# Three sets of norm scales loaded at the start into one 48-row tile and turned by one transpose

## The chip, the cores and the metric

The kernel runs on one core of one Trainium2 chip. The metric is the device time of one execution in microseconds (us); for the kernel before it is the median of three runs. Beside them stands one more execution that the hardware profiler recorded, and every duration, wait and queue below is from that one.

The core has five engines that run their own instruction streams and wait for each other by semaphores: PE (TensorE, matrix products and transposes; its weight loads are shown apart as PEld), DVE (VectorE), ACT (ScalarE), POOL (GpSimd) and SP (SyncE, which here issues nearly all loads). A transfer is issued by an instruction on SP or ACT and then carried by the core's 16 DMA engines.

## The reference

The kernel computes two layers of a decoder trunk for one sequence of 256 tokens, width 1024, in float32. Each layer is

```
h = x + 1/2 * SwiGLU_1(RMSNorm(x) * g1)
h = h + mixer(RMSNorm(h) * g2)      # three attention groups, one combined projection
y = h + 1/2 * SwiGLU_2(RMSNorm(h) * g3)
```

`RMSNorm(x) * g` is `x * rsqrt(mean(x*x) + 1e-6) * g`, with a scale vector `g` of 1024 numbers. There are three such vectors for each layer, named `ffn1_norm`, `mix_norm` and `ffn2_norm`, each an array of 2 x 1024 for the two layers. The hidden width of each SwiGLU is 2816. The mixer takes the normalised rows through a projection, attends in 4 + 4 + 8 heads of width 64, and projects back.

## The kernel before, in words

**Layout.** The trunk `h` stays in SBUF as `trunk`, with tokens on the 128 partitions, in two halves of 128 tokens. For a product the activations must lie with the 1024 columns on the partitions. `Norm` does that: for each block of 128 columns PE transposes the two token halves into a PSUM bank (`turn`, L338; in the first layer's opening a `turn` of its own, L495), ACT writes the rounded high part to `xhl` while it multiplies by the norm scale (`Norm.high`, L327), and DVE writes the remainder of it (`Norm.low`, L330). The row factor `rsqrt(...)` is applied later, behind the product.

**The scales.** After the transpose a scale belongs to a partition, so ACT and DVE take it as one number per partition from `gT`, a tile of 128 partitions and 48 columns: column `16 * which + 8 * layer + block`. To get there, `load_gains` (L175) loads one of the three arrays as 16 rows of 128 numbers (two layers by eight blocks) into a temporary tile, and `turn_gains` (L179, L180) transposes these rows on PE into a PSUM bank and copies 16 columns into `gT` on DVE.

**Weights.** Weights are loaded in 1 MB pieces into `raw` (L92, five buffers), split by ACT into a high part `wh` (L118) and by DVE into a low part `wl` (L122), both of type float32r. Every product then is three matmuls: high by high, high by low, low by high (L303). The issue of a load waits on SP until its `raw` buffer is free.

**A feed-forward block** (`ffn`) runs over 22 tiles of 128 hidden columns. Each tile f has a gate and an up product, held by a `Pair` in two PSUM banks of the tag `gu`. There are four banks of that tag, given out in turn. ACT and DVE drain them (L441, L442), and DVE and ACT compute the gated value (L446, L448, L465, L466, L453, L456, L459). The down product of tile f - 4 runs between the products of tile f. Odd and even tiles take their wide (high) and narrow (low) matmuls in opposite order, so that the narrow matmuls of one even tile and of the next odd tile stand beside each other on PE.

**Order.** The program is scheduled by hand: each engine executes its instructions in the order in which the Python code emits them. Semaphores are inserted by the framework from the tiles that instructions read and write.

**The start.** On PE the order is: six warm-up products on a tile of ones (`warm_up(WARM)`, 12 matmuls in the trace), the first transpose of scales (`turn_gains(0)`), the four transposes of the first 256 columns of x (`turn(0)`), three more warm-up products (`warm_up(BRIDGE)`), and then the first products of `opening`, which take the weights in quarter and half pieces as they arrive. On SP the loads are issued in the order x columns 0 to 255, the first quarter of the gate weights, the first of the up weights, x columns 256 to 511, and so on. ACT issues one load, `ffn1_norm`, and then loads its table and runs an `Exp` on a tile of ones (L195), so that the table is there when it is needed.

**The other two sets.** `load_small` is called at tile f = 4 of the first feed-forward block and puts four loads on SP: the constants, `mix_norm`, `ffn2_norm` and the forget bias. `before_mixer`, called at f = 8 behind the products of that tile, turns the two sets by two transposes, each with its own `gu` bank, ahead of the narrow matmuls of f = 9, and puts two copies into `gT` on DVE, ahead of a few more small preparations for the mixer.

The tiles `rows` come from the pool `tmp`, nine buffers that the feed-forward blocks use for their intermediate values; a buffer is given out again when its last use is past.

Of the kernel before, what the change touches and what calls it, by code (L numbers as in the profile page):

```python
# [18 lines left out]
P = 128  # L19
# [123 lines left out]
def kernel(ctx: ExitStack, tc: tile.TileContext, x, ffn1_norm, ffn1_w_gate, ffn1_w_up, ffn1_w_down,  # L143
                      mix_norm, w_in, forget_bias, a_q_norm, a_k_norm, b_q_norm, b_k_norm, c_q_norm, c_k_norm,
                      w_out, ffn2_norm, ffn2_w_gate, ffn2_w_up, ffn2_w_down, const, out):
    nc = tc.nc
# [12 lines left out]
    V, A, G, T = nc.vector, nc.scalar, nc.gpsimd, nc.tensor  # L159

    def bank(tag):
        return psum.tile([P, 512], F32, name="ps_" + tag, tag=tag)

    def tmp(n):
        return tp.tile([P, 512], F32, name="tmp", tag="tmp")[:, :n]
# [2 lines left out]
    trunk = xp.tile([P, 2, D], F32, name="trunk")  # L168
    cst = cp.tile([P, 512], F32, name="cst")
    ident = cp.tile([P, P], F32, name="ident")  # L170
    rows = [tmp(P)[:16] for _ in range(3)]
    gT = cp.tile([P, 48], F32, name="gT")

    def load_gains(i, g, eng):
        eng.dma_start(rows[i], g.rearrange("l (k p) -> (l k) p", p=P))  # L175

    def turn_gains(i):
        ps = bank("gu")
        T.transpose(ps[:, :16], rows[i], ident[:16, :16])  # L179
        V.tensor_copy(gT[:, 16 * i:16 * i + 16], ps[:, :16])  # L180

    ones = cp.tile([P, P], F32, name="ones")
    G.memset(ones, 1.0)  # L183
# [5 lines left out]
    def load_x(mp):  # L189
        cols = slice(256 * mp, 256 * mp + 256)  # L190
        nc.sync.dma_start(trunk[:, :, cols], x[0].rearrange("(t p) d -> p t d", p=P)[:, :, cols])

    load_x(0)
    load_gains(0, ffn1_norm, nc.scalar)
    A.activation(tmp(P), ones, AF.Exp)  # L195

    def head_gains(l):
# [81 lines left out]

    def load_small():  # L280
        nc.sync.dma_start(cst, const)
        load_gains(1, mix_norm, nc.sync)
        load_gains(2, ffn2_norm, nc.sync)
        nc.sync.dma_start(fb, bass.AP(tensor=forget_bias.tensor, offset=forget_bias.offset,
                                      ap=[[0, P], [8, DEPTH], [1, 8]]))

# [94 lines left out]
    def ffn(norm, nxt, aside=None, first=False):  # L381
# [189 lines left out]
        for f in range(1, NF):  # L571
# [32 lines left out]
            if f == 4 and first:  # L604
                load_small()
# [37 lines left out]
    def mixer_tables(l):  # L643
        gb = head_gains(l)
        for i in range(4):
            g = gb[:, i]
            if i % 2 == 0:
                G.tensor_tensor(gq, g, eighth, op=ALU.mult)
                g = gq
            gs = g[:, None, :].to_broadcast([P, 2, HD])  # L650
            G.tensor_tensor(tab[:, i, 0], cs[:, :, 0:64], gs, op=ALU.mult)
            G.tensor_tensor(tab[:, i, 1, :, 0:32], cs[:, :, 64:96], gs[:, :, 32:64], op=ALU.mult)
            G.tensor_tensor(tab[:, i, 1, :, 32:64], cs[:, :, 96:128], gs[:, :, 0:32], op=ALU.mult)
        G.tensor_tensor(gc, gb[:, 4], gb[:, 5], op=ALU.mult)
        G.tensor_tensor(gc, gc, eighth, op=ALU.mult)
# [528 lines left out]

    def before_mixer(l):
        if l == 0:
            turn_gains(1)
            turn_gains(2)
            V.tensor_copy(identr, ident)
            V.memset(causal[:, P:2 * P], 0.0)  # L1190
            for t in range(2):
                V.tensor_scalar(causal[:, 2 * t * P:(2 * t + 1) * P], future, NEG, None, op0=ALU.mult)
        mixer_tables(l)
# [6 lines left out]

    warm_up(WARM, True)
    norm = Norm(0, 0)
    turn_gains(0)
    for l in range(DEPTH):
        norm = ffn(norm, lambda: Norm(1, l), lambda: before_mixer(l), l == 0)
        norm = mixer(l, norm, lambda: Norm(2, l))
        norm = ffn(norm, (lambda: Norm(0, l + 1)) if l + 1 < DEPTH else None)
# [35 lines left out]
```

## Time and profile before

| | |
|---|---|
| median of three runs | 1037.53 us (1037.35 to 1038.41) |
| the profiled execution, own time | 1037.25 us |
| its span, first to last instruction | 1035.5 us |
| PE busy | 1031.3 us, 5641 matmuls |
| DVE busy | 808.0 us |
| ACT busy | 592.1 us |
| POOL busy | 147.3 us |
| moved by DMA | 181.61 MB, mean 175 GB/s |

The profiled execution's own time is 1.75 us longer than its span, which covers what lies ahead of the first and behind the last instruction. In the timeline a row gives start, length, engine, line, operation, the tile written and the tiles read, and in brackets how long the engine had been idle and what ended that. An engine name with a q at its end (SPq, ACTq) is the instruction that issues a transfer, not the transfer. PEld rows are weight loads, which run ahead of the matmul they belong to. Matmuls are pipelined: the start of the next one, not the end of the last, tells the pace.

### The profile page before, as it was taken

What the parts mean: (1) busy time and instruction counts of PE and PEld (TensorE: products, weight loads), DVE (VectorE), ACT (ScalarE), POOL (GpSimd) and SP (SyncE); (2) the same over time, 40 slices, a digit from 0 to 9 for tenths busy, and PEclk for the clock granted to TensorE, in tenths of its full rate; (3) what the DMA queues carried; (4) which work ended last, traced back from release to release, by engine and by line L of the source; (5) the groups of instructions that cost most, each with busy time, mean ns of one, the idle gap of its engine ahead of it and who ended that gap; (6) DMA issues with size and microseconds to landing.
All of it is one profiled execution on the core that took longest, in us unless ns stands there. A gap on an engine that the chain in (4) does not pass through costs nothing.

```text
span 1035.5 us, 15082 instructions
## 1 busy us (share of the span) xinstructions
PE 1031.3 (100%) x5641; PEld 898.4 (87%) x5641; DVE 808.0 (78%) x1537; ACT 592.1 (57%) x1045; POOL 147.3 (14%) x177
## 2 busy tenths in 40 slices
PE   9999999999999999999999999999999999999998
PEld 8888888898888888888888888888988988888887
DVE  6977778789876877777788777787898768777776
ACT  6655556666854655555465555557676646555552
POOL 2003000167800000000000110002766000000000
PEclk9999999999999999999999999999999999999999
DMA  9664656554431364645645564664455224564631
GB/s 324 224 240 162 208 188 198 182 191 170 158 127 42 123 230 150 230 168 203 198 163 193 182 224 146 241 186 172 164 195 170 83 69 160 180 204 162 236 130 41
DMA packets 130808, 181.61 MB, mean 175 GB/s; under 512 B 7040, under 2 KB 104624, under 8 KB 130736
## 3 DMA queue, kind: packets, MB, share of 16 engines
q1 hardware_dynamic: 130704, 180.66, 51.3%
q8 instruction: 44, 0.72, 0.3%
q14 instruction: 28, 0.23, 0.1%
q10 hardware_dynamic: 32, 0.01, 0.0%
HBM read 179.60 MB, written 1.05 MB: 174 GB/s over the span
## 4 chain that ended last, share of the span: by engine, by line
PE 100%; DVE 0%; POOL 0%; issue 0%; POOLq 0%
PE ps_gu L303 66%; PE ps_acc L303 30%; PE ps_acc L338 1%; PE ps_gu L1037 1%; PE ps_gu L1140 1%; PE ps_acc L738 0%; PE ps_acc L1037 0%; PE ps_gu L1070 0%; PE ps_acc L495 0%; PE ps_acc L364 0%; PE ps_acc L1070 0%; PE ps_gu L179 0%; DVE trunk L377 0%; POOL ones L183 0%; POOL minus_half L185 0%
## 5 line engine op out<-in xcount | busy, mean ns | idle before, releaser
L122 DVE TENSOR_TENSOR wl<-raw,wh 128x1024 fp32r<-128x1024 f32 (+2 forms) x342 | 417.0, 1225 | 24.7 <-ACT wh L118 24.7
L118 ACT CAST wh<-raw 128x1024 fp32r<-128x1024 f32 (+2 forms) x341 | 343.1, 1036 | 5.4 <-PE ps_gu L303 4.8
L303 PE MATMUL ps_gu<-xhl,wh 128*128 128x512 f32 x1408 | 330.2, 390 | 0.0
L303 PEld LDWEIGHTS ps_gu<-xhl,wh 128*128 128x128 f32 x1408 | 262.7, 188 | 53.8 <-ACT wh L118 0.3
L303 PEld LDWEIGHTS ps_gu<-xhl,wl 128*128 128x128 f32 x1408 | 176.0, 191 | 4.3 <-issue 0.2
L303 PE MATMUL ps_gu<-xhl,wl 128*128 128x256 f32 x1408 | 179.2, 283 | 0.1
L303 PE MATMUL ps_gu<-wh,xhl 128*128 128x512 f32 (+2 forms) x512 | 157.2, 377 | 0.0
L442 DVE TENSOR_TENSOR tmp<-ps_gu,tmp 128x256 f32<-128x256 f32 x176 | 73.0, 423 | 107.8 <-ACT tmp L441 107.5
L303 PE MATMUL ps_acc<-wh,hh 128*128 128x512 f32 (+1 forms) x352 | 137.2, 390 | 0.0
L303 PE MATMUL ps_acc<-wl,hh 128*128 128x512 f32 (+1 forms) x352 | 137.0, 389 | 0.0
L303 PE MATMUL ps_acc<-wh,hl 128*128 128x512 f32 (+1 forms) x352 | 136.5, 388 | 0.0
L441 ACT COPY tmp<-ps_gu 128x256 f32<-128x256 f32 x176 | 63.5, 371 | 93.5 <-PE ps_gu L303 93.2
L303 PEld LDWEIGHTS ps_gu<-wh,xhl 128*128 128x128 f32 x512 | 94.8, 188 | 14.6
L456 ACT CAST hh<-tmp 128x256 fp32r<-128x256 f32 x80 | 32.6, 407 | 119.7 <-DVE tmp L453 119.7
L303 PE MATMUL ps_gu<-wl,xhl 128*128 128x512 f32 (+2 forms) x256 | 95.7, 374 | 0.0
L448 ACT ACTIVATE tmp<-tmp 128x256 f32<-128x256 f32 x88 | 36.9, 419 | 82.3 <-DVE tmp L446 81.9
L314 POOL TENSOR_TENSOR y_n<-msq,minus_half 128x2 f32<-128x2 f32 x6 | 6.8, 1141 | 530.9 <-DVE msq L313 530.9
L303 PEld LDWEIGHTS ps_acc<-wh,hl 128*128 128x128 f32 x352 | 66.1, 188 | 13.9
L303 PEld LDWEIGHTS ps_acc<-wh,hh 128*128 128x128 f32 x352 | 66.2, 188 | 12.6
L303 PEld LDWEIGHTS ps_acc<-wl,hh 128*128 128x128 f32 x352 | 66.2, 188 | 12.2
L303 PEld LDWEIGHTS ps_gu<-wl,xhl 128*128 128x128 f32 x256 | 48.2, 188 | 6.7
L327 ACT ACTIVATE xhl<-ps_acc,gT 128x256 fp32r<-128x256 f32 x48 | 19.1, 474 | 38.7 <-PE ps_acc L338 35.6
(221 smaller groups left out, 1000.4 us busy)
## 6 DMA issues: line engine op xcount, KB each, us to landing
raw<-in_ffn_w_down_dram SPq DMA_DIRECT2D x44, 1024.0 KB, 4.9
raw<-in_ffn_w_gate_dram SPq DMA_DIRECT2D x42, 1024.0 KB, 6.6
raw<-in_ffn_w_up_dram SPq DMA_DIRECT2D x42, 1024.0 KB, 7.3
raw<-in_w_in_dram SPq DMA_DIRECT2D x24, 1024.0 KB, 4.9
raw<-in_w_out_dram SPq DMA_DIRECT2D x8, 1024.0 KB, 4.9
raw<-in_w_in_dram SPq DMA_DIRECT2D x4, 768.0 KB, 4.9
raw<-in_w_in_dram SPq DMA_DIRECT2D x4, 656.0 KB, 3.9
raw<-in_ffn_w_gate_dram SPq DMA_DIRECT2D x3, 512.0 KB, 7.0
```

Of the source, the lines that this page charges most:

```text
L118: self.nc.scalar.copy(hv, src)
L122: (engine or self.nc.vector).tensor_tensor(lv, self.srcs[self.n_low], hv.bitcast(F32), op=ALU.subtract)
L303: T.matmul(o, l, r, start=start, stop=stop, skip_group_check=True)
L314: G.tensor_tensor(y, dst, minus_half[:, :n], op=ALU.pow)
L327: A.activation(self.h[:, m], src, AF.Copy, scale=gT[:, self.col + m:self.col + m + 1])
L338: T.transpose(ps[:, i, t * P:(t + 1) * P], trunk[:, t, (2 * mp + i) * P:(2 * mp + i + 1) * P], ident)
L441: A.copy(o, ps[:, 1])
L442: V.tensor_tensor(o, ps[:, 0], o, op=ALU.add)
L448: A.activation(th, t_, AF.Tanh, scale=0.5)
L456: (V.tensor_copy if late else A.copy)(hh, t_)
L1037: T.transpose(b[:, j * P:(j + 1) * P], pj[i][:, j * P:(j + 1) * P], ident)
L1140: T.transpose(b[:66, i * S + t * P:i * S + (t + 1) * P], src[t][:, 2 * hp_ + i, :], ident)
```

## The change

The three temporary tiles of 16 rows become one of 48 rows. All three loads are issued by ACT at the start, one behind the other, ahead of the table load. One transpose of 48 rows and one copy of 48 columns take the place of three of each, at the place of the first. The two loads in `load_small` and the two turns in `before_mixer` go away.

```diff
-    rows = [tmp(P)[:16] for _ in range(3)]
+    rows = tmp(P)[:48]
     gT = cp.tile([P, 48], F32, name="gT")

     def load_gains(i, g, eng):
-        eng.dma_start(rows[i], g.rearrange("l (k p) -> (l k) p", p=P))
-
-    def turn_gains(i):
+        eng.dma_start(rows[16 * i:16 * i + 16], g.rearrange("l (k p) -> (l k) p", p=P))
+
+    def turn_gains():
         ps = bank("gu")
-        T.transpose(ps[:, :16], rows[i], ident[:16, :16])
-        V.tensor_copy(gT[:, 16 * i:16 * i + 16], ps[:, :16])
+        T.transpose(ps[:, :48], rows, ident[:48, :48])
+        V.tensor_copy(gT, ps[:, :48])
...
     load_x(0)
-    load_gains(0, ffn1_norm, nc.scalar)
+    for i, g in enumerate((ffn1_norm, mix_norm, ffn2_norm)):
+        load_gains(i, g, nc.scalar)
     A.activation(tmp(P), ones, AF.Exp)
...
     def load_small():
         nc.sync.dma_start(cst, const)
-        load_gains(1, mix_norm, nc.sync)
-        load_gains(2, ffn2_norm, nc.sync)
...
         if l == 0:
-            turn_gains(1)
-            turn_gains(2)
             V.tensor_copy(identr, ident)
...
-    turn_gains(0)
+    turn_gains()
```

## The prediction

> **What bounds the kernel now.** I read the profile's page first: the engines' busy times and the chain that ended last.
>
> ```profile
> span 1035.5 us, 15082 instructions
> ...
> PE 1031.3 (100%) x5641; PEld 898.4 (87%) x5641; DVE 808.0 (78%) x1537; ACT 592.1 (57%) x1045; POOL 147.3 (14%) x177
> ...
> PE 100%; DVE 0%; POOL 0%; issue 0%; POOLq 0%
> ```
>
> PE is busy in 1031.3 of 1035.5 us and the chain is PE from end to end. So a wait anywhere else costs nothing by itself; what counts is how late PE starts, how long it stands, and how many instructions it has. The change touches PE at two places only, and the first one is the start. The timeline of the first microseconds:
>
> ```profile
> 0.78 0.46 ACTq L175 DMA_DIRECT2D tmp<-in_ffn_norm_dram  x1
> ...
> 0.79 0.43 SPq L191 DMA_DIRECT2D trunk<-in_x_dram  x1
> ...
> 1.04 2.93 PE L303 MATMUL ps_gu<-ones 128*128 128x128 f32 x12 [1.04 <-POOL minus_half L185]
> ...
> 1.27 1.28 ACT L195 ACT_TABLE_LOAD   x1 [1.27 <-PEq L1231]
> 1.27 0.46 SPq L92 DMA_DIRECT2D raw<-in_ffn_w_gate_dram  x1
> ...
> 1.78 0.46 SPq L92 DMA_DIRECT2D raw<-in_ffn_w_up_dram  x1
> ...
> 2.56 0.31 ACT L195 ACTIVATE tmp<-ones 128x128 f32<-128x128 f32 x1
> ...
> 3.90 0.18 PEld L179 LDWEIGHTS ps_gu<-ident,tmp 16*128 16x128 f32 x1 [0.22 <-issue]
> ...
> 4.11 0.71 PEld L495 LDWEIGHTS ps_acc<-ident,trunk 128*128 128x128 f32 x4
> ...
> 4.22 0.17 DVE L180 COPY gT<-ps_gu 128x16 f32<-128x16 f32 x1 [4.22 <-PE ps_gu L179]
> 4.60 0.61 POOL L478 CAST wh<-raw 128x512 fp32r<-128x512 f32 x1 [2.88 <-DMA raw<-in_ffn_w_gate_dram]
> ...
> 4.84 0.90 ACT L327 ACTIVATE xhl<-ps_acc,gT 128x256 fp32r<-128x256 f32 x2 [1.97 <-PE ps_acc L495]
> ...
> 5.35 0.91 DVE L330 SCALAR_TENSOR_TENSOR xhl<-ps_acc,gT,xhl 128x256 fp32r<-128x256 f32 x2 [0.95 <-ACT xhl L327]
> ...
> 5.95 0.76 PEld L303 LDWEIGHTS ps_gu<-xhl,wh 128*128 128x128 f32 x4
> ```
>
> Read it from PE. The warm-up products (1.04) are there to fill the time until data arrive. The weight load of the scale transpose follows at 3.90, that of the x transposes at 4.11. ACT takes the first x block at 4.84, when its transposes are through, DVE adds the low part at 5.35, and the first product starts at 5.95. Each of these steps stands behind the transpose of the scales in PE's queue, so what holds that transpose holds everything. When did its data come? The views of the loads, of the transpose's own line, and of the tile `trunk` (whose last line gives the time from issue to landing of its four loads) say:
>
> ```profile
> tmp<-in_ffn_norm_dram ACTq DMA_DIRECT2D x1, 8.0 KB, 2.5
> tmp<-in_mix_norm_dram SPq DMA_DIRECT2D x1, 8.0 KB, 6.5
> tmp<-in_ffn_norm_dram SPq DMA_DIRECT2D x1, 8.0 KB, 6.2
> ```
>
> ```profile
> L179 PEldq EVENT_SEMAPHORE  x3: 51/51/51, 3.4 to 69.6; - x3
> ```
>
> ```profile
> DMA to landing us min/median/max: 3.0/5.3/5.7
> ```
>
> The scales issued at 0.78 landed 2.5 us later, at 3.28; PE's semaphore wait for them ended from 3.40 to 3.45, 0.17 us behind the landing. The first x block, with the shortest of the four landings, 3.0, came at 0.79 + 3.0 = 3.79. Both were there when the warm-up was done. The scale load is covered by the warm-up and by x, with 3.90 - 3.45 = 0.45 us to spare.
>
> The second place is the pair of turns at tile f = 8. The chain of waits in order of time, around the opening and around that place (start, length, what):
>
> ```profile
> 4.18 1.04 PE ps_acc L495 x4
> ...
> 7.66 0.44 PE ps_acc L495 x4
> ...
> 53.45 3.83 PE ps_gu L303 x32
> ...
> 70.01 1.91 PE ps_gu L303 x16
> 71.92 0.22 PE ps_gu L179 x2
> 72.14 2.11 PE ps_gu L303 x16
> ```
>
> The row of 53.45 is the narrow matmuls of tiles f = 6 and 7, 32 of them in 3.83 us. At f = 8 and 9 the same 32 stand in two rows with the two scale transposes between: 70.01 to 74.25 is 4.24 us. The two turns cost 0.41 us of PE there: 0.22 for themselves, and 0.20 by which the 16 matmuls behind them take 2.11 instead of 1.91.
>
> **The change part by part.**
>
> *Three loads at the start.* SP issues its loads 0.48 to 0.51 apart (0.79, 1.27, 1.78). ACT at the same pace would issue its three at 0.78, 1.28 and 1.79, and the one transpose now waits for the third. For its time to land the nearest row is the 2.5 us of the same size on the same queue at the same stage. The far end is the 6.5 us of the same size on SP's queue, behind a megabyte of weights. Between them lies the first quarter of the gate weights, 32 times the bytes: issued at 1.27, used by POOL at 4.60, at most 3.3. I take 2.6, near the row that is nearest, a little more because the DMA engines are busier than when the first load went out. The third set lands at 1.79 + 2.6 = 4.39, PE can go at 4.39 + 0.17 = 4.56, and that is 0.66 later than 3.90. The spare 0.45 is already used in this. With 2.5 it would be 0.56, with 3.3 it would be 1.36.
>
> *What is queued behind that wait.* On PE the four x transposes and all the products: they shift by the 0.66, since x (3.79) is there by then and is no longer what is late. On DVE the copy into `gT` and the low parts, on ACT the high parts; these follow PE. The weight splits on POOL and ACT hang on DMA instead and keep their times.
>
> *ACT's own queue.* Two more issues push the table load and the Exp by 1.79 - 0.78 = 1.01 us: the table load from 1.27 to 2.28, the Exp's end from 2.87 to 3.88. ACT's next instruction comes at 4.84 (then 5.5) after 1.97 us of idling. Cost nothing; if the cover were gone it would be up to 1.01.
>
> *One transpose of 48 rows.* Its matmul has 48 columns instead of 16. The chain has 1.04 us for the four x transposes of 128 columns of that moment, 2 ns a column; 32 more are 0.06, taken as 0.05 because part of it lies under the next weight load. The copy of 48 columns runs on DVE beside the x transposes (4.22 against the 4.84 at which it is first used): nothing.
>
> *Two turns less at f = 8.* PE gets back 0.41 us as worked out above: 0.22 at the least, if the slower matmuls behind have another cause. A likely cause of the 0.20 is the banks: the two turns each take one of four, so that f = 9 gets the two that f = 8 has just filled, and which ACT and DVE are still draining; without the turns it gets those of f = 7.
>
> *Two loads less on SP and two copies less on DVE.*
>
> ```profile
> 40.58 0.42 SPq L175 DMA_DIRECT2D tmp<-in_mix_norm_dram  x1
> ...
> 41.05 0.91 SPq L175 DMA_DIRECT2D tmp<-in_ffn_norm_dram  x1
> ...
> 49.56 0.39 SPq L92 DMA_DIRECT2D raw<-in_ffn_w_down_dram  x1
> ```
>
> ```profile
> 78.60 0.24 DVE L180 COPY gT<-ps_gu 128x16 f32<-128x16 f32 x2
> ...
> 78.90 0.38 ACT L441 COPY tmp<-ps_gu 128x256 f32<-128x256 f32 x1 [0.43 <-PE ps_gu L303]
> ```
>
> SP is free 0.42 + 0.91 us sooner, but its next weight load comes at 49.56, when a buffer is free, so only the forget bias is earlier. DVE's two copies (0.24 us) go; behind them stand preparations for the mixer and a drain of tile f = 9, and PE does not stand at that place. The two `tmp` buffers that the sets held until f = 8 come free early; no wait for a `tmp` buffer is on PE's chain. POOL issues and loses nothing. All these: nothing.
>
> *What the opening can give back.* PE has one visible wait of its own later in the opening, which hangs on a weight load and not on the scales:
>
> ```profile
> 12.89 2.35 DVE L122 TENSOR_TENSOR wl<-raw,wh 128x1024 fp32r<-128x1024 f32 x2
> ...
> 13.97 0.77 PEld L303 LDWEIGHTS ps_gu<-xhl,wh 128*128 128x128 f32 x4 [0.30 <-ACT wh L118]
> ...
> 14.78 1.13 PEld L303 LDWEIGHTS ps_gu<-xhl,wl 128*128 128x128 f32 x8
> ```
>
> The 0.30 us at 13.97 could swallow part of the shift. But the narrow matmuls of 14.78 need the low parts that DVE makes from 12.89 to 15.24, behind the low parts of x, which shift. So I count 0, and 0.30 as the other end.
>
> *Sum.* 0.66 + 0.05 - 0.41 = +0.30 us on the profiled execution, 1037.25 to 1037.55. Ends of the terms: 0.56 + 0 - 0.41 - 0.30 = -0.15, and 1.36 + 0.05 - 0.22 = +1.19. The profiled execution lies 0.28 below the median of the runs, so on that scale the forecast is 1037.83, its own range with the scatter of the runs 1037.1 to 1038.9. A change of 0.2% (2.07 us) is about what a measurement of this kernel can tell from none, so this is no measurable change.
>
> **Rival 1, slower: the three loads go one after the other.** They write into one tile where before there were three. If the framework orders writes to one tile, whatever their rows, ACT issues the second only when the first has landed: at 3.45, landing 5.95 and seen at 6.12; the third lands at 8.62, PE goes at 8.79, 4.89 later, and the sum is 4.89 + 0.05 - 0.41 = +4.5 us, 1042.1. With 6.5 us each it would be about 1050. Against it: the four x loads write one tile in different columns and SP issues them without waits; but these are columns, and no row of this trace has loads into different partitions of one tile. From a third landing at 6.16 on (PE 2.43 late) this decides against the change. Chance 8 in 100.
>
> **Rival 2, slower: a pause in the warm-up keeps PE slow for longer.** Weight loads between 5.2 and 5.4 and between 6.0 and 6.3, grouped by form, and the first stretch of five microseconds with the granted clock as its third number from the end:
>
> ```profile
> L303 PEld LDWEIGHTS ps_gu<-ones 128*128 128x128 f32 x2 | 0.5, 333 | 0.0
> ```
>
> ```profile
> L303 PEld LDWEIGHTS ps_gu<-xhl,wh 128*128 128x128 f32 x2 | 0.3, 188 | 0.0
> ```
>
> ```profile
> 0.00:5.00 5.00, 3.96 (x17) 3.70 (x18) 0.17 (x1) 1.75 (x3) 1.49 (x15) 1.00 0.53 167
> ```
>
> The granted clock shows 1.00 throughout, yet the weight loads of one shape take 333 ns and then 188, and the four x transposes 1.04 us at 4.18 and 0.44 at 7.66: PE is slow from 1.04 to about 5.5. The change puts a pause of some 0.7 us into these 4.5 us. If they begin anew at 4.56, PE is slow until 9.1, 3.6 us more, and loses 3.6 x (1 - 188/333) = 1.6 us to 3.6 x (1 - 0.44/1.04) = 2.1: a sum of +1.9 to +2.4, 1039.4 to 1039.9. Against it: PE already pauses 0.22 us ahead of 3.90 and speeds up all the same. Chance 10 in 100, half of it above 0.2%. [...]
>
> **Rival 3, slower: the third load lands as late as the ones on SP did.** With 6.2 to 6.5 us it lands at 8.0 to 8.3, the shift is 4.3 to 4.6, the sum +3.9 to +4.2, 1041.4 to 1041.7. For it: the weights on SP's queue are issued at 1.27 and 1.78, ahead of the third set. Against: the first set, issued 0.01 us ahead of x, overtook it (2.5 against 3.0). Chance 4 in 100. [...]
>
> **Rival 4, the shift is swallowed.** The 0.30 at 13.97 and earlier readiness of other parts take it, and the turns at f = 8 are pure gain: -0.41 to 0, 1037.1 to 1037.5. For it: splits and loads do not shift. Chance 12 in 100.
>
> **How the numbers follow.** Forecast 66, rival 4 12, rival 2 10, rival 1 8, rival 3 4 in 100. The time is the forecast's, 1037.8. The range goes from rival 4 less the scatter of the runs, 1036.9, to the middle of rival 2, 1039.7, and leaves out rivals 1 and 3 and part of 2. Within 0.2%: 66 + 12 + 5 = 83, less 1 for what I do not see; slower 8 + 4 + 5 = 17; faster 1 in 100, since no case gives it.
>
> **What would show it.** ACT issues at 0.78, about 1.28 and 1.79, with no wait between; the weight load of the scale transpose at about 4.5 to 4.6, released by a load; the first product at about 6.6; slow weight loads until about 5.5; no gap at f = 8, where 32 narrow matmuls run in 3.83; the last matmul about 0.3 later. It is wrong if the second issue on ACT comes behind 3 us, if the third set takes over 3.3 us to land, or if PE makes up or loses anything between 20 us and f = 8.

## The result: 0.14% slower, in three groups of executions

The median of 22 executions of the changed kernel is 1039.19 us; 22 of the kernel before, beside them, have 1037.47. The ratio is 1.0014, with a 95% interval of 1.0007 to 1.002. So the kernel became slower by 1.5 us (by the ratio) to 1.7 us (by the medians). That is within the 0.2% to which the prediction gave 82 in 100, and inside its range, but not at its 1037.8.

The single times say more than the median. The kernel before lies between 1037.1 and 1038.4. The changed one lies in three groups: four executions from 1037.5 to 1037.7, fifteen from 1038.7 to 1039.6, three from 1040.4 to 1040.6. The profiled execution took 1037.56 and belongs to the smallest times. Its span is 1035.8, only 0.3 longer than before. Its time is the forecast's 1037.55 to the tenth, but it does not show what most executions do.

**The profile after (1037.56).** The timeline of the start:

```profile
1.27 0.47 ACTq L175 DMA_DIRECT2D tmp<-in_mix_norm_dram  x1
...
1.77 0.49 ACTq L175 DMA_DIRECT2D tmp<-in_ffn_norm_dram  x1
...
2.29 1.28 ACT L196 ACT_TABLE_LOAD   x1 [2.29 <-issue]
...
5.33 0.13 PEld L179 LDWEIGHTS ps_gu<-ident,tmp 48*128 48x128 f32 x1 [1.65 <-POOL wh L477]
5.36 0.23 PE L179 MATMUL ps_gu<-ident,tmp 48*128 48x48 f32 x1 [1.39 <-DMA tmp<-in_ffn_norm_dram]
...
5.51 0.42 PEld L494 LDWEIGHTS ps_acc<-ident,trunk 128*128 128x128 f32 x4
...
7.10 0.76 PEld L302 LDWEIGHTS ps_gu<-xhl,wh 128*128 128x128 f32 x4 [0.45 <-issue]
```

The three issues on ACT come at 0.78, 1.27 and 1.77, with no wait between them. The transpose of the scales starts at 5.33 instead of 3.90, and the first product at 7.10 instead of 5.95. Its weight load takes 0.13 us and the four of the x transposes 0.42, where before they took 0.18 and 0.71: PE was already at its higher speed when the wait ended, and that gave back some of the delay (1.43 us at the transpose, 1.15 at the first product). The chain of waits of the same execution, and two rows of the kernel before to set beside it:

```profile
1.77 3.45 DMA tmp<-in_ffn_norm_dram
...
34.95 2.72 PE ps_acc L302 x12
...
54.22 3.83 PE ps_gu L302 x32
...
70.77 3.83 PE ps_gu L302 x32
74.61 2.75 PE ps_acc L302 x12
```

```profile
34.18 2.72 PE ps_acc L303 x12
...
74.25 2.75 PE ps_acc L303 x12
```

The third set took 3.45 us to land. The down product that began at 34.18 begins at 34.95, 0.77 later; the one behind tile f = 9 at 74.61 instead of 74.25, 0.36 later. Between them the 32 narrow matmuls of f = 8 and 9 take 3.83, as those of f = 6 and 7 do: the two turns gave back their 0.41. So the sum of this execution is the forecast's, but not its steps: the transpose came 1.43 us late instead of 0.66, 0.77 more than forecast, and the opening gave back 1.43 - 0.77 = 0.66, which the forecast had at nothing. The agreement to the tenth is luck, and it does not explain the 1039.19.

### The profile page after: what moved, and what is told of

It is laid out like the page before. It is cut to its first block, busy times and chain, and to the rows that moved or that the text cites. A ratio compares the mean times of both kernels' runs of the same rounds, so it can differ in the third digit from the quotient of the medians.

```text
span 1035.8 us, 15070 instructions
## 1 busy us (share of the span) xinstructions
PE 1030.0 (99%) x5639; PEld 897.4 (87%) x5639; DVE 807.8 (78%) x1535; ACT 591.5 (57%) x1045; POOL 148.5 (14%) x177
## 4 chain that ended last, share of the span: by engine, by line
PE 99%; DMA 0%; ACTq 0%; DVE 0%; ACT 0%; issue 0%
PE ps_gu L302 66%; PE ps_acc L302 30%; PE ps_acc L337 1%; PE ps_gu L1036 1%; PE ps_gu L1139 1%; DMA tmp<-in_ffn_norm_dram 0%; PE ps_acc L737 0%; PE ps_acc L1036 0%; PE ps_gu L1069 0%; PE ps_acc L494 0%; ACTq L175 0%; PE ps_acc L1069 0%; PE ps_acc L363 0%; DVE xhl L329 0%; ACT xhl L326 0%
```

## The experiments

Two theories were set against each other. *Theory P*: the pause of PE ahead of the transpose keeps PE slow for longer in most executions (the prediction's rival 2). *Theory L*: the third set of scales lands at different times (a form of rival 3). Nearly every kernel ran eleven times, beside the kernel before on the same chip, whose median stands with each.

### A profile of the larger group

The changed kernel itself, no edit.

> The changed kernel once more, for the spread of its executions and for a profile of one of the longer ones. So far the 22 executions of the changed kernel lie in three groups, near 1037.6, near 1039.2 and near 1040.5, while the profiled one (1037.56) is from the first group and shows the scale transpose at 5.33. Theory P (the pause of PE ahead of the transpose keeps PE slow for longer in most executions): a profile of a longer execution has the scale transpose at 5.2 to 5.4 as well, but weight loads of 333 ns and x transposes of 1.04 us for four until 7 to 9, and all of the 1.5 us is lost before 15. Theory L (the third set of scales lands at different times): the scale transpose comes 1.5 us later, at about 6.9, with weight loads of 188 ns behind it. Either way nothing changes behind 20 us, and 32 narrow matmuls at tiles f = 8 and 9 take 3.83 us.

Measured: median 1039.01 against 1037.47, ratio 1.0015 (1.0007 to 1.0024). One execution lay near 1037.7, eight between 1038.8 and 1039.3, two near 1040.3. The profiled one took 1039.17. Its weight loads on PE, then two rows of its chain, then the stretch from 5 to 10 us with the granted clock third from the end:

```profile
1.04 2.64 PEld L302 LDWEIGHTS ps_gu<-ones 128*128 128x128 f32 x12 [1.04 <-POOL minus_half L185]
5.28 0.18 PEld L179 LDWEIGHTS ps_gu<-ident,tmp 48*128 48x128 f32 x1 [1.60 <-issue]
5.55 0.71 PEld L494 LDWEIGHTS ps_acc<-ident,trunk 128*128 128x128 f32 x4
...
7.53 1.40 PEld L302 LDWEIGHTS ps_gu<-xhl,wh 128*128 128x128 f32 x4
9.02 1.18 PEld L302 LDWEIGHTS ps_gu<-xhl,wl 128*128 128x128 f32 x4
10.15 0.53 PEld L494 LDWEIGHTS ps_acc<-ident,trunk 128*128 128x128 f32 x4
```

```profile
36.62 2.72 PE ps_acc L302 x12
...
76.28 2.75 PE ps_acc L302 x12
```

```profile
5.00:10.00 5.00, 4.69 (x18) 4.24 (x19) 1.72 (x4) 1.41 (x3) 2.51 (x3) 1.00 1.00 319
```

The scale transpose starts at 5.28, no later than in the shorter execution. But now PE is slow: 0.18 and 0.71 for the weight loads that took 0.13 and 0.42, then 1.40 for four loads at 7.53 that took 0.76 there, and 1.18 for four still at 9.02. At 10.15 four x transposes load in 0.53: the higher speed has come. At the down product of 34.18 the lag is 36.62 - 34.18 = 2.44 us, against 0.77 in the shorter execution; behind f = 9 it is 76.28 - 74.25 = 2.03. All of the difference between the two executions, 2.44 - 0.77 = 1.67 us there and 1.61 in their times, arises in the opening. Theory P holds, theory L does not for this pair. The granted clock of the stretch reads 1.00, as in the same stretch of the kernel before and of the profile after: PE's speed in the opening has to be read from durations of one shape.

The same kernel was profiled once more later.

> The changed kernel once more, for one more profile. If it falls among the executions near 1039 it shows the scale transpose at 5.2 to 6.3 and slow weight loads (over 290 ns) until 9 to 10, as in the profile at 1039.17; if it falls near 1040.4, slow weight loads for some 1.2 us more, or a later landing of the third set by as much; if near 1037.6, weight loads of 188 ns from the scale transpose on.

Measured: eight executions, one at 1037.62, the others from 1038.6 to 1039.6, median 1039.34 against 1037.37, ratio 1.0014 (1.0004 to 1.0024). The profile fell on 1039.22:

```profile
5.67 0.18 PEld L179 LDWEIGHTS ps_gu<-ident,tmp 48*128 48x128 f32 x1 [2.00 <-POOL wh L477]
...
7.92 1.40 PEld L302 LDWEIGHTS ps_gu<-xhl,wh 128*128 128x128 f32 x4
9.42 0.86 PEld L302 LDWEIGHTS ps_gu<-xhl,wl 128*128 128x128 f32 x4
10.22 0.46 PEld L494 LDWEIGHTS ps_acc<-ident,trunk 128*128 128x128 f32 x4
```

The same picture: slow from 5.67 until after 9.42. Here the third set came 0.4 later, and the time is the same 1039.2. Over the three series 41 executions of the changed kernel make 6 near 1037.6, 30 between 1038.6 and 1039.6, and 5 above 1040. Two of the 30 were profiled, and both show the slow PE; that the others do too is read from their times. The last group was never caught in a profile; what it is stays open.

### The wait alone

```diff
 # kernel before: three tiles, three turns
-    load_gains(0, ffn1_norm, nc.scalar)
+    for i, g in ((1, mix_norm), (2, ffn2_norm), (0, ffn1_norm)):
+        load_gains(i, g, nc.scalar)
...
-        load_gains(1, mix_norm, nc.sync)
-        load_gains(2, ffn2_norm, nc.sync)
```

> The kernel before with one thing of the change alone, the wait: three tiles, three turns at their old places, all sets loaded by ACT at the start, but the set that the first turn needs is issued third. So the first transpose, still of 16 rows, waits for a load issued at 1.77, and the turns at tile f = 8 stay. Theory P (the pause ahead of the transpose keeps PE slow for longer): the same three groups of executions as the changed kernel, 0.4 us later because the 0.41 at f = 8 is not won: median 1039.4 to 1039.6. If instead the 48-row tile or the 48-row transpose were the cause: 1037.3 to 1037.9.

Measured: 1039.71 against 1037.22, ratio 1.0018 (1.0009 to 1.0027), one execution at 1037.94 and the others from 1038.8 to 1040.6. Weight loads of the profile (1039.87), and rows of its chain:

```profile
6.30 0.18 PEld L179 LDWEIGHTS ps_gu<-ident,tmp 16*128 16x128 f32 x1 [2.62 <-POOL wh L477]
...
8.49 1.27 PEld L302 LDWEIGHTS ps_gu<-xhl,wh 128*128 128x128 f32 x4
9.80 0.66 PEld L302 LDWEIGHTS ps_gu<-xhl,wl 128*128 128x128 f32 x4
```

```profile
1.78 4.41 DMA tmp<-in_ffn_norm_dram
...
72.66 1.91 PE ps_gu L302 x16
74.57 0.22 PE ps_gu L179 x2
74.79 2.11 PE ps_gu L302 x16
```

Neither the 48-row tile nor the 48-row transpose is in this kernel, and it has the whole loss: 2.5 us, where the changed kernel's 1.7 and the 0.41 not won at f = 8 (1.91 + 0.22 + 2.11) make 2.1. The median is 0.1 above the expected range. The third set took 4.41 us to land this time, so the landing does vary, from 3.45 to 4.41 between the profiles of the kernels that wait for it.

### The loads alone

```diff
 # kernel before: three tiles, three turns
-    load_gains(0, ffn1_norm, nc.scalar)
+    for i, g in enumerate((ffn1_norm, mix_norm, ffn2_norm)):
+        load_gains(i, g, nc.scalar)
...
-        load_gains(1, mix_norm, nc.sync)
-        load_gains(2, ffn2_norm, nc.sync)
```

> The load part of the change alone: all three sets are loaded by ACT at the start, but into three tiles, and the three turns stay where they were, so that the first one waits for the first load only. Theory P: PE has no pause, the first scale transpose is at 3.9, median 1037.5, within 0.2 of before. Theory L in the form that the extra loads slow the others (x, first weights) would give 1038 or more.

Measured: 1037.25 against 1037.47, ratio 0.9998 (0.9989 to 1.0007), all eleven between 1037.0 and 1037.6. The line of the scale transposes, with their first start, and the loads of the first two groups of x transposes in the profile (1037.25):

```profile
L179 PEld LDWEIGHTS ps_gu<-ident,tmp x3: 133/137/167, 3.9 to 71.9; 16*128 16x128 f32 x3
```

```profile
4.09 0.42 PEld L494 LDWEIGHTS ps_acc<-ident,trunk 128*128 128x128 f32 x4
...
7.41 0.42 PEld L494 LDWEIGHTS ps_acc<-ident,trunk 128*128 128x128 f32 x4 [0.27 <-DMA trunk<-in_x_dram]
```

The three loads and the later table load cost nothing that can be measured. What costs is that the first transpose waits for the last of them (1039.71 in the run above).

Two more things can be read here. Without any long pause PE was already fast at 4.09 (0.42 for four loads), while in the kernel before it was slow there (0.71) and until about 5.5: the moment of the speed-up differs between executions. And the early speed won nothing, since PE then stood 0.27 for the second block of x, and the down product began at 34.20, as in the kernel before (34.18). In these two executions a slow PE cost nothing, since the work ahead of that block was done when it landed, at about 7.4.

### The pause filled

```diff
 # changed kernel
-WARM = 6
+WARM = 10
```

> The changed kernel with 10 warm-up products instead of 6, so that PE has work until about 5.2, when the third set has landed (5.22 in the profile after). The work is wasted either way; only the pause goes. Theory P: the executions near 1039.2 and 1040.5 disappear, all lie at 1037.3 to 1038.2, median about 1037.6. Theory L: the spread stays, median about 1039.2.

Measured: 1038.05 against 1037.47, ratio 1.0004 (0.9996 to 1.0013); ten executions from 1037.3 to 1038.4, one at 1039.15. Weight loads of the profile (1037.62):

```profile
1.04 3.64 PEld L302 LDWEIGHTS ps_gu<-ones 128*128 128x128 f32 x20 [1.04 <-POOL minus_half L185]
5.39 0.14 PEld L179 LDWEIGHTS ps_gu<-ident,tmp 48*128 48x128 f32 x1 [0.71 <-POOL wh L477]
5.58 0.42 PEld L494 LDWEIGHTS ps_acc<-ident,trunk 128*128 128x128 f32 x4
```

The larger group is all but gone, with the scales as late as ever (5.39). So of the changed kernel's 1.5 to 1.7 us about one is the slow PE (1039.19 - 1038.05 = 1.14). The median is 0.45 above the expected 1037.6. Whether the late transpose costs more in most executions than in the profile after, or PE is still slow for a part of them, is not shown: the profile fell on one of the shortest. The filling was not complete either, since in this execution PE sped up during the warm-up (20 weight loads in 3.64, where 12 took 2.63 in the profile after), finished it at 4.68, and paused 0.71.

### A pause without a late load

```diff
 # kernel before
-WARM = 6
+WARM = 2
```

> The kernel before with 2 warm-up products instead of 6: loads, turns and waits are those of before, but PE pauses from about 1.9 to 3.5, as long a pause as in the changed kernel. Theory P: most executions become longer by 1 to 2.5 us, median 1038.5 to 1040. Theory L: nothing lands later, so the median stays at 1037.5, or comes 0.2 lower since the transpose can start at 3.45 instead of 3.90.

Measured: 1037.99 against 1037.47, ratio 1.0003 (0.9995 to 1.0012), spread from 1037.3 to 1038.9. That is half a microsecond longer than before, not the 1 to 2.5 expected, and the interval takes in no change: this run alone does not show that a pause costs time. Weight loads of the profile (1037.68):

```profile
1.03 0.93 PEld L303 LDWEIGHTS ps_gu<-ones 128*128 128x128 f32 x4 [1.03 <-POOL minus_half L185]
3.41 0.18 PEld L179 LDWEIGHTS ps_gu<-ident,tmp 16*128 16x128 f32 x1 [1.45 <-issue]
...
5.80 1.19 PEld L303 LDWEIGHTS ps_gu<-xhl,wh 128*128 128x128 f32 x4
7.04 0.66 PEld L303 LDWEIGHTS ps_gu<-xhl,wl 128*128 128x128 f32 x4
```

PE stops at 1.96, resumes at 3.41, and is slow until about 6.7, against about 5.5 in the kernel before. The slow stretch is there, but the pause lay earlier: PE resumed 1.9 us sooner than in the changed kernel and was fast before the second block of x was there. That block took 5.6 us to land instead of 5.1, and PE stood 0.19 for it at 7.89; so of the 0.49 by which the down product is late (34.67) only a part is the slow PE. The expectation counted the pause's length and left out its place.

### A shorter wait

```diff
 # changed kernel
-        load_gains(i, g, nc.scalar)
+        load_gains(i, g, nc.sync if i == 2 else nc.scalar)
```

> The changed kernel with half the wait: the third set goes out on SP, behind the first x block at 1.27, instead of third on ACT at 1.77. It should land at about 4.3 and the transpose start at 4.4, a pause of PE's weight loads of 0.75 instead of 1.65. SP's weight loads go out 0.5 later. Theory P in its simple form (the longer the pause, the longer PE stays slow): fewer executions near 1039, median 1037.6 to 1038.3. If any pause at all is enough: median about 1038.8, the groups still there. If the later weight loads bind, at most 0.5 more.

Measured: 1037.41 against 1037.22, ratio 1.0 (0.9991 to 1.0009), all from 1037.1 to 1038.1, no groups. Weight loads of the profile (1037.43):

```profile
4.13 0.18 PEld L179 LDWEIGHTS ps_gu<-ident,tmp 48*128 48x128 f32 x1 [0.46 <-issue]
4.41 0.71 PEld L494 LDWEIGHTS ps_acc<-ident,trunk 128*128 128x128 f32 x4
5.11 0.91 PEld L302 LDWEIGHTS ps_gu<-ones 128*128 128x128 f32 x6
6.58 0.76 PEld L302 LDWEIGHTS ps_gu<-xhl,wh 128*128 128x128 f32 x4 [0.56 <-POOL wh L477]
```

```profile
tmp<-in_ffn_norm_dram SPq DMA_DIRECT2D x1, 8.0 KB, 2.5
```

Issued on SP right behind x, at 1.27, the third set took 2.5 us and landed at about 3.8, half a microsecond sooner than expected, in time for a transpose at 4.13; the pause was 0.46 and did no harm: the six loads at 5.11 take 0.91, the next four 0.76. This keeps the one tile, the one transpose and all loads at the start, at no measurable cost. It gains nothing either, since the first product is still 0.6 late (6.58 against 5.95).

### Scales behind x on PE

```diff
 # changed kernel
             xT = turn(0)
+            turn_gains()
             warm_up(BRIDGE)
...
-    turn_gains()
```

> The changed kernel with the transpose of the scales behind the four x transposes on PE instead of ahead of them: x is there at 3.8, so PE works until 4.8 and pauses only 0.5, the scales are turned at 5.3 as before, and ACT takes x at about 5.7 instead of 6.0. Theory P: the group near 1039 gets rare, median 1037.4 to 1038.0. If what costs is the late scale and not the slow PE: only 0.3 better than the changed kernel, 1038.7 to 1039.

Measured: 1039.23 against 1037.22, ratio 1.0014 (1.0006 to 1.0023), two executions near 1037.5, nine from 1038.8 to 1039.7. Weight loads of the profile (1039.32):

```profile
4.01 0.71 PEld L494 LDWEIGHTS ps_acc<-ident,trunk 128*128 128x128 f32 x4 [0.34 <-issue]
5.94 0.18 PEld L179 LDWEIGHTS ps_gu<-ident,tmp 48*128 48x128 f32 x1 [1.21 <-issue]
...
9.12 1.18 PEld L302 LDWEIGHTS ps_gu<-xhl,wl 128*128 128x128 f32 x4
10.25 0.54 PEld L494 LDWEIGHTS ps_acc<-ident,trunk 128*128 128x128 f32 x4
```

The expectation of theory P failed here by its size of the pause. The x transposes ended at 4.72 and the third set was seen only at 5.9, so the pause was 1.21, not 0.5. And it was as harmful as the 1.6 of the changed kernel: slow until after 9.12. The median alone lies nearer to the other case (1038.7 to 1039); it is the weight loads that speak for the slow PE. The pause of 0.46 was harmless and this one of 1.21 was not; what decides it between them, the length or the moment, no run here shows.

### Versions without the wait

```diff
 # kernel before
-    rows = [tmp(P)[:16] for _ in range(3)]
+    first, rest = tmp(P), tmp(P)
+    rows = [first[:16], rest[:16], rest[16:32]]   # all loaded by ACT at the start
...
-            turn_gains(1)
-            turn_gains(2)
+            turn_gains(rest, 16, 32)
+            for _ in range(3):
+                bank("gu")
```

> A version without the wait: all sets loaded by ACT at the start, the first one into a tile of its own and turned alone at the start; the other two share a tile of 32 rows and one transpose at f = 8, and the bank count there is padded to four, so that f = 9 gets the banks of f = 7 as it does at every other tile. Expected: first transpose at 3.9, no pause; at f = 8 the 32 narrow matmuls and one transpose take 3.83 + 0.11 = 3.94 instead of 4.24 if the banks are the cause of the 0.20, 4.14 if they are not. Median 1037.0 to 1037.2 against 1037.47 of before.

Measured: 1037.21 against 1037.22, ratio 0.9998 (0.999 to 1.0007). Rows of the chain at f = 8 and 9, and the narrow matmuls around that place, shortest, median and longest in ns:

```profile
69.78 1.91 PE ps_gu L303 x16
71.69 0.18 PE ps_gu L180
71.87 2.11 PE ps_gu L303 x16
```

```profile
L303 PE MATMUL ps_gu<-xhl,wl x23: 279/283/384, 70.7 to 73.7; 128*128 128x256 f32 x23
```

One transpose instead of two saved 0.04, not the 0.3 expected: it costs 0.18, and the 16 matmuls behind it still take 2.11, with the banks kept apart. So the banks are not the cause of the 0.20. One narrow matmul takes 384 ns instead of 283, the first behind the transpose; that is half of the 0.20, and the rest was not traced.

The second version takes that transpose away from f = 8 as well:

```diff
 # the version above
-            turn_gains(rest, 16, 32)
...
                 xT = turn(2 * m + 1)
+                if m:
+                    turn_gains(rest, 16, 32, "acc")   # copied to gT by ACT
```

> The version without the wait once more, with the second turn (32 rows, mix_norm and ffn2_norm) moved from tile f = 8 into the opening, behind the last x transposes, into a bank of the other tag, and its copy on ACT. There PE has a wait of 0.30 of its own for a weight split soon after, which should take the 0.18 to 0.38 that the transpose costs. Expected: first scale transpose at 3.9; 32 narrow matmuls at f = 8 and 9 in 3.83; span 0.0 to 0.4 shorter than before (1035.1 to 1035.5), median 1036.8 to 1037.2 beside 1037.2 to 1037.5 of before; too little to be told apart from none for certain.

Measured: 1036.94 against 1037.37, ratio 0.9997 (0.9988 to 1.0006), all eleven from 1036.6 to 1037.3. Rows of the chain:

```profile
11.54 0.20 PE ps_acc L180
...
69.93 3.83 PE ps_gu L303 x32
```

The turn at 11.54 takes 0.20 in the opening, of which nothing is left at the down product (34.11, in the kernel before 34.18), and f = 8 and 9 run at the pace of every other pair, 3.83. The sign fits the 0.41, but the interval takes in no change, so this is not shown to beat the kernel before.

## Why the prediction was right in its range and wrong in its middle

*The terms.* The issues on ACT (0.78, 1.27, 1.77 for 0.78, 1.28, 1.79) came as worked out, and ACT's shifted table load cost nothing (the loads alone). The transpose of 48 rows took 0.31 us on a slow PE (the profile of 1039.17), the one of 16 rows 0.25 (the wait alone): the 0.05 was about right. The two turns gave back 0.41, as forecast; their copies, SP's two loads and the two `tmp` buffers cost or won nothing that shows. The reason offered for the 0.20 in the 0.41, the banks, was wrong, as the split version showed.

*The landing.* Taken as 2.6 us, with 3.3 as the upper bound of the forecast, it was 3.45 in the profile after and 4.41 in the longest. So in the profile after the shift of the transpose was 1.43, not 0.66. The step that failed is the choice of the row: the nearest load, the 2.5 of the first set, was issued together with the first x block, the third behind 0.5 MB of x and weights, with another 0.25 MB 0.02 us after it. The gate quarter, at most 3.3, was the better row, and even that was short. The third set was also behind two loads of ACT's own; no run separates the two, and the 2.5 us of the set issued on SP at 1.27 fits both.

*The opening.* I counted 0 for what it gives back. In the profile after, the 1.43 of the transpose became 1.15 at the first product, since PE was fast by then, and 0.77 at 34 us, mostly since the wait of 0.30 at 13.97 was gone. In the shorter wait on SP it gave back nothing: 0.63 at the first product, 0.63 at the down product (34.81). The end of 0.30 was about the right size for what comes behind the first product, in one of the two. In the profile after, the landing that was taken too short and the return that was left out cancelled each other.

*The likeliest case.* It was the wrong one. Rival 2 had 10 in 100 and a time of 1039.4 to 1039.9; 30 of 41 executions lie at 1038.6 to 1039.6, and the two of them that were profiled show it. Its price came out: from 1037.6 to 1039.2 is 1.6 us, the lower of the two prices, made from weight loads of 333 and 188 ns. That is in part luck, since PE stayed slow until about 10.1 in the profile of 1039.17, not until 9.1, while the fast execution beside it stood idle for 0.45 and 0.17 us among its first products, which the slow one did not. What failed is the argument against it, that PE already paused 0.22 us and sped up all the same. The pause of the forecast was 0.7, the real one 1.6; a run with 0.46 lost nothing measurable (1037.41 against 1037.22) and one with 1.21 lost 2.0 us (1039.23 against 1037.22). A harmless short pause said nothing about a long one. Whether it is the length alone that counts stays open.

*The other rivals.* The loads did not go one after the other: the issues on ACT stand 0.50 apart. A landing as late as the old ones on SP did not come, but its direction was right. What the range held, it held by reaching up to rival 2.

## What to carry to other kernels

A transpose that gathers several small loads waits for the last of them, and where it stands at the head of the critical engine's queue this delay reaches everything behind it (1.43 us at the transpose, 0.77 still at 34 us in the shortest profile); loads can be early and gathered, while the one that is needed first keeps a step of its own (1037.21 against 1037.22 in the first version without the wait). A pause of the critical engine can cost more than its length: in the profile of 1039.17 one of 1.60 us made the down product 2.44 late, and 1.67 of these were not lost in the execution of the same kernel in which PE was fast behind a pause of 1.65. And where executions fall in groups, one profile shows one group: read the single times before the profile.

## What the runs showed of the hardware

PE's speed in the first ten microseconds was not set by the work alone. Two executions of one program, idle from about 3.7 to 5.3, came out of that pause with weight loads of 0.13 and of 0.18 us for one shape. Behind pauses of 2.62, 1.45 and 1.60 us PE stayed slow for another 3.3 to 4.8 us (from 6.30 to about 9.6 in the wait alone, from 3.41 to about 6.7 in the pause without a late load, from 5.28 to about 10.1 in the profile of 1039.17). Without a long pause it was fast from about 4 in one execution (0.42 for four loads at 4.09, the loads alone) and from about 5.5 in another (333 ns a load between 5.2 and 5.4, 188 between 6.0 and 6.3, the kernel before). In the filled pause it was still fast behind 0.71 us of idling (0.14 at 5.39). What sets the moment of the speed-up, and why the same pause put it off in one execution and not in another, is not shown; the granted clock reads 1.00 in the first 15 us of the kernel before and of the changed kernel's profiles of 1037.56 and 1039.17.

The same 8 KB took 2.3 to 2.8 us to land when issued first, at 0.78, and 3.45 to 4.41 when issued a microsecond later, third on ACT and behind x and weights (3.45 in the profile after, 3.52 in the filled pause, 4.07 with the scales behind x, 4.41 in the wait alone).
